# New costs for transfers in a source's list scheduler, other product orders in the middle down stages, and small work moved to another stage

## The chip, the cores and the metric

The kernel runs on one core of a Trainium2 chip. The core has five engines that run side by side, each with its own list of instructions: PE (matrix products into PSUM, a small memory of eight banks), DVE (element-wise work), ACT (element-wise work, copies, activation functions), POOL and SP. Here SP issues the loads of the weights and POOL issues a few transfers that add one on-chip buffer to another. The metric is the time of one execution on the device, in microseconds (us).

## The reference

One layer of a decoder block over 256 tokens of width 2048, in float32:

```
def swiglu_ffn(x, w_gate, w_up, w_down):
    return (jax.nn.silu(x @ w_gate) * (x @ w_up)) @ w_down
...
x = x + 0.5 * swiglu_ffn(rms_norm(x, ffn1_norm), ffn1_w_gate, ffn1_w_up, ffn1_w_down)
z = rms_norm(x, mix_norm) @ w_in
...
a = jnp.exp(-8 * r * jax.nn.softplus(-lam))
...
x = x + y @ w_out
x = x + 0.5 * swiglu_ffn(rms_norm(x, ffn2_norm), ffn2_w_gate, ffn2_w_up, ffn2_w_down)
return rms_norm(x, final_norm)
```

The gate and up weights of an FFN are 2048 x 5632, the down weight is 5632 x 2048. Between the two FFNs lies a mixer (a gated linear recurrence and a short convolution); its vector `softplus(-lam)` and a few others depend on parameters alone and are worked out once by `prepare()`.

## The kernel before

**Products in float32.** A weight block of 512 x 512 (1 MB) is loaded to a buffer `raw`, then split in two parts that PE can multiply: ACT casts `hi` (two instructions of 128x1024), DVE subtracts to get `lo`. Each block is multiplied as `hi` x (both parts of the activations) and `lo` x (the high part). PE needs `hi` first and `lo` right after it.

**Seven products for eight.** Two units of 512 rows and two column blocks form a 2 x 2 matrix of blocks w11, w12, w21, w22, and a scheme after Strassen and Winograd makes its result with seven products p0 to p6 of sums of blocks: p0 uses w11, then w11 takes in w12 (p4), then w22 (p5), then w21 (p3); p6 uses w12 + w22, p2 uses w22 and p1 w21. Two of the sums (w12 += w22 and, in the middle down stages, w11 += w21) are made by POOL transfers, `by_transfer`; the others are DVE additions into the buffer. Beside the seven, ordinary units x01, x11, x00, x10 multiply two more row units; the second digit is the column block. Results gather in PSUM banks named a, c, d, e (and f), each one a 128 x 512 quadrant or part of it. ACT's snapshots of a bank are u2, u3, s5; its copy d<-a (`seed`) lets a bank go on from another's sum. `hs` are sums of activations that some products use; `ph` are PE transposes of a unit of hidden values, and `h` the parts made from them.

**Stages.** Each FFN runs: a first gate/up block; `down(False)`, the down product of units 0, 1, 2 (column block c = 0 as ordinary units d_1_0, then blocks 1 and 2 by seven products, then c = 3 as ordinary units 3_0, 3_2, 3_1, used on PE in that order of 0 first); a fine gate/up stage (g1, u1, g2, u2); `down_stage`, the middle down stage, in two passes d_2_0 and d_2_1 of two column blocks each; a second fine stage (g3, u3, g4, u4); `down(True)`. The number before the first underscore in a name is the FFN: `d1_2_0` is FFN1's middle down stage, pass 0.

**What sets the order.** The fine and middle down stages are laid out by a list scheduler in the source, class `Plan`, that runs when the program is written. A step has an engine, a length, a tail (time until its result is there), and needs; PE's order is fixed by the caller (`usual_order`, `orders`), SP's follows from when a load is late, and the rest is chosen by earliest start and urgency. Loads choose a buffer (`room`) by when its last reader is done; `finish` hands those times to the next stage's plan. In these stages the instructions are pinned to the written order. The other stages are ordered by the framework from dependencies, with the order of the source as priority. For c = 3 of `down(False)` the buffers are named by hand: `chosen["raw"]` gives raw3 to 3_0, which held w11 (last read by p3's split); raw4 held w12 (last read by p6's split). In the buffer rooms of the two layouts, "three" (raw0 to raw4) and "fine" (kept, tall, short), the same memory is used again.

`prepare()` first runs `turns` (two PE transposes, `pv_many` and `pv_conv`, of small parameter rows, each copied by DVE to `cols_many`, `cols_conv`), then on ACT `lam_abs` and `lam_exp` (the latter with another activation table, so an ACT_TABLE_LOAD ahead of it), then some 20 DVE instructions on 128x8 values (`lam_den`, `lam_s`, `lam_poly`, `sp2`, `sn4` and others).

All instructions that go through the wrapper `Engine` have line L43 in the profile, so groups are told apart by names: the profile writes `hi_d_p` for `hi` of a product of a down stage, `hi_d_x` for that of an ordinary unit there, `hi_d` for that of the single units of `down`, `ps_d_a` for a bank, `raw_d_w` for a buffer.

Of the kernel before, what the change touches and what calls it, by code (L numbers as in the profile page):

```python
# [48 lines left out]
class Step:  # L49

    def __init__(self, engine, length, fn, needs, tail, due, at):
        self.engine, self.length, self.fn, self.tail, self.due, self.at = engine, length, fn, tail, due, at
        self.needs = [n for n in needs if n is not None]
        self.late = self.start = self.end = None
        self.room, self.readers = None, []


class Plan:
# [15 lines left out]

    def load(self, length, fn, room, tail=2.3):
        step = self.add("SP", length, fn, tail=tail)
        step.room = room
        return step
# [50 lines left out]
    def run(self):  # L129
# [6 lines left out]
        while True:  # L136
# [37 lines left out]
def hybrid_block(ctx: ExitStack, tc: tile.TileContext, a: dict, out: bass.AP):  # L174
# [94 lines left out]
    turns = []  # L269
# [464 lines left out]
    def ffn(tag, norm, after, opening=False):  # L734
        with tc.tile_pool(name=f"ffn{tag}", bufs=1, side="left", reuse_waits="tile") as fp:
# [304 lines left out]
            def down(last):  # L1040
# [11 lines left out]
                def finish(c, ps):  # L1052
                    y = [keep(f"y_{t}") for t in range(NT)]
                    for t in range(NT):
# [4 lines left out]
                        else:  # L1059
                            for h in range(2):  # L1060
# [3 lines left out]
                                close(t, y[t], h, 2)  # L1064

                for c in (0, 3):
                    if c == 3:
                        chosen["pair"].extend([1, 0, 1, 2][4 - len(us) :])
                        if len(us) == 3:
                            chosen["raw"].extend([3] + [i for i in recent["raw"] if i in (1, 2)])  # L1070
                    end = last and tag == 2 and c == NC_D - 1
# [11 lines left out]
                    if c == 0:  # L1083
# [192 lines left out]
            def fetch(plan, w, cs, runs, name, rooms):  # L1276
                got = {}

                def run(room):
                    rows = sum(n for _, n in runs)  # L1280
                    raw = got["raw"] = pools[room].tile([P, rows, CW], F32, tag="raw", name=f"raw_{name}")
                    at = 0
                    for k, n in runs:
                        sp.dma_start(raw[:, at : at + n, :], w[k * P : (k + n) * P, cs].rearrange("(j p) c -> p j c", p=P))
                        at += n

                step = plan.load(sum(n for _, n in runs) * 0.73, run, rooms)
                return step, lambda: got["raw"]
# [30 lines left out]

            def sevens(plan, w, cs, name, sf, rows, xs, rooms, order, pairs, result, turned4=False, fills=None, apart=False):  # L1320

# [51 lines left out]
                def unit(key):  # L1373
# [13 lines left out]
                    elif key == "p3":  # L1387
                        last = made["p5"].lo[-1]
                        if turned4:
                            sources = [by_transfer("w11", "w21", last, loads["w21"])]  # L1390
# [20 lines left out]
                for key in units_only:  # L1411
                    for n in {"p0": "a", "p5": "a", "p6": "a", "p3": "a", "p4": "f" if apart else "c", "p2": "c", "p1": "d"}.get(key) or (
                        "ec" if key[2] == "1" else "da"
                    ):
                        last_on[n] = key
                wait_for = {
                    (1, 1): ("e", ["u3"] if apart else ["u3", "s5"]), (0, 1): ("c", ["u2"]), (1, 0): ("a", []), (0, 0): ("d", []),
                }
# [8 lines left out]
                for key in order:  # L1427
# [7 lines left out]
                    if key[0] == "x":  # L1435
# [15 lines left out]
                    needs = {5: ["seed"], 6: ["u2"], 3: ["u3"], 2: [] if apart else ["s5"], 1: ["seed"]}.get(q, [])  # L1451
                    u.over(to(b), lambda q=q: sf[q], q in (0, 4), *[made[z] for z in needs], *((fills or {}).get(q, [])))
                    u.under((to(b), lambda q=q: sf[q], q in (0, 4, 5, 6) or last_on[b] == key))
# [60 lines left out]
            def down_result(plan, cols, later, then=None):  # L1514
                def result(t, n, ps, done, keys, snaps, made):
# [58 lines left out]
            def down_stage(s, free, ready, tails, later):  # L1574
# [55 lines left out]
                pairs = [0, 1, 2] * 5 + [0, 1, 2, 1, 0, 1, 2]  # L1630
                orders = [list(usual_order), usual_order[:8] + ["p3", "p1", "x10"]]
                orders[0] = ["x01", lambda: turn_cells(plan, cells, turned), "p0", "x11", "p4", "p1", "p5", "p6", "x00", "p2", "p3", "x10"]
                for i, cols in enumerate(((2 * CW, CW), (3 * CW, 0))):

                    class Late(dict):
# [8 lines left out]
                        plan, wd, cols, f"d{tag}_{s}_{i}", sh, rows, xs, rooms, orders[i], pairs[11 * i : 11 * i + 11],  # L1644
                        down_result(plan, cols, handed if i else None), turned4=True, fills=fills,
                        apart=i == 0,
                    )
# [15 lines left out]
            for s in (1, 3):  # L1663
# [29 lines left out]
    def prepare():  # L1693
        for t in turns:
            t()

        lam = vec["lru_lambda"]
# [479 lines left out]
```

## Time and profile before

| | us |
|---|---|
| Time, median of 3 runs | 1751.11 |
| Lowest and highest | 1747.46, 1751.56 |
| The profiled execution's own time | 1748.15 |
| Its span | 1746.4 |
| PE busy | 1715.0 (98%) |
| DVE busy | 1530.6 (88%) |
| ACT busy | 1096.0 (63%) |
| Mean granted PE clock | 0.996 |

In the timelines below a row is: start, length, engine, line, operation, result <- operands, tile and shape, how many were joined, and in brackets the idle time of the engine before it with what ended it. `SPq` and `POOLq` are the issuing of transfers, and a transfer's row gives its size and the median time from issue to landing. In a table by windows, each engine has its busy time and instructions, and then come the granted clock (1.00 is full speed), the busy share of the DMA engines and the rate.

### The profile page before, as it was taken

To read this page: it belongs to the slowest core of one execution; us is meant where nothing else is said; L and a number is where in the kernel's file an instruction comes from. 1 tells how busy PE (TensorE), PEld (TensorE's weight loads), DVE (VectorE), ACT (ScalarE), POOL (GpSimd) and SP (SyncE) were. 2 spreads that over 40 slices of the span, in tenths; PEclk is the share of its full clock that TensorE was granted. 3 is DMA by queue.
4 is the path that set the end of the run, shared out by engine and by line. 5 is a ranking of instruction groups with operands and counts; after the bars stand their busy time and mean duration, and the time that the engine had idled before them with its cause. 6 is when DMAs were issued, how large, how long until landed. Compare 5 with 4: busy or idle time off the path is not lost. (4 is left out here: it accounts for less than half of the span.)

```text
span 1746.4 us, 20389 instructions
## 1 busy us (share of the span) xinstructions
PE 1715.0 (98%) x7913; PEld 1420.4 (81%) x7913; DVE 1530.6 (88%) x1320; ACT 1096.0 (63%) x1346; POOL 50.8 (3%) x84
## 2 busy tenths in 40 slices
PE   9999999999899999999999999999999999999998
PEld 8888888887688888888888888787888877878886
DVE  7989899997799987887897888788899998999976
ACT  7666566665566655667865666565566565666654
POOL 0100000000000000000000000000000000000000
PEclk9999999999999999999999999999999999999999
DMA  8775976868777865655566675665777877877663
GB/s 299 235 223 165 290 226 221 262 175 268 219 230 226 264 194 193 230 168 183 179 199 207 209 251 158 194 239 152 242 246 229 262 211 233 271 251 227 226 197 121
DMA packets 182450, 383.09 MB, mean 219 GB/s; under 512 B 7509, under 2 KB 10449, under 8 KB 177873
## 3 DMA queue, kind: packets, MB, share of 16 engines
q1 hardware_dynamic: 174656, 340.81, 56.5%
q0 software_dynamic: 7520, 39.92, 11.8%
q8 instruction: 62, 1.02, 0.2%
q10 hardware_dynamic: 176, 1.06, 0.1%
q14 instruction: 36, 0.29, 0.0%
HBM read 339.82 MB, written 2.10 MB: 196 GB/s over the span
## 5 line engine op out<-in xcount | busy, mean ns | idle before, releaser
L43 ACT CAST hi_g_p<-raw_g_w 128x1024 fp32r<-128x1024 f32 x112 | 138.9, 1262 | 85.3 <-DVE raw_g_w L43 36.9
L43 ACT CAST hi_u_p<-raw_u_w 128x1024 fp32r<-128x1024 f32 x112 | 138.3, 1261 | 77.6 <-PE ps_u_a L43 25.8
L43 DVE TENSOR_TENSOR lo_g_p<-raw_g_w,hi_g_p 128x2560 fp32r<-128x2560 f32 (+2 forms) x72 | 159.7, 2227 | 18.8 <-PE ps_d L43 9.7
L43 DVE TENSOR_TENSOR lo_u_p<-raw_u_w,hi_u_p 128x2560 fp32r<-128x2560 f32 (+2 forms) x72 | 159.0, 2227 | 9.6 <-ACT hi_u_p L43 5.9
L43 PE MATMUL ps_in<-xT_nm,hi_in 128*128 128x512 f32 x512 | 122.5, 391 | 0.0
L43 PE MATMUL ps_d<-hi_d,h 128*128 128x512 f32 x440 | 107.0, 396 | 5.0 <-ACT hi_d L43 5.0
L43 PEld LDWEIGHTS ps_in<-xT_nm,hi_in 128*128 128x128 f32 x512 | 94.1, 188 | 18.8 <-ACT tha L43 0.5
L43 PEld LDWEIGHTS ps_d<-hi_d,h 128*128 128x128 f32 x440 | 83.1, 190 | 22.9 <-ACT hi_d L43 5.8
L43 DVE TENSOR_TENSOR lo_in<-raw_in,hi_in 128x2048 fp32r<-128x2048 f32 x32 | 73.2, 2289 | 20.8 <-ACT hi_in L43 20.3
L43 ACT CAST hi_in<-raw_in 128x1024 fp32r<-128x1024 f32 x64 | 64.3, 1047 | 33.6 <-PE ps_in L43 18.2
L43 ACT CAST hi_d<-raw_d 128x1024 fp32r<-128x1024 f32 x56 | 55.5, 1046 | 40.9 <-PE ps_d_d L43 11.5
L43 ACT CAST hi_d_p<-raw_d 128x1024 fp32r<-128x1024 f32 x56 | 56.4, 1046 | 31.6 <-DVE raw_d L43 16.8
L43 DVE TENSOR_TENSOR raw_u_w<-raw_u_w,raw_u_w 128x1024 f32<-128x1024 f32 (+2 forms) x40 | 69.6, 1757 | 6.8 <-DMA raw_u_w<-in_ffn_w_up_dram 5.8
L43 DVE TENSOR_TENSOR lo_d_p<-raw_d,hi_d_p 128x2048 fp32r<-128x2048 f32 x28 | 63.4, 2285 | 10.9 <-ACT hi_d_p L43 10.7
L43 DVE TENSOR_TENSOR lo_d<-raw_d,hi_d 128x2048 fp32r<-128x2048 f32 x28 | 63.6, 2287 | 9.4 <-ACT hi_d L43 9.3
L43 DVE TENSOR_TENSOR lo_d_p<-raw_d_w,hi_d_p 128x2048 fp32r<-128x2048 f32 (+1 forms) x36 | 64.7, 1812 | 6.7 <-ACT hi_d_p L43 6.7
L43 DVE TENSOR_TENSOR raw_g_w<-raw_g_w,raw_g_w 128x1024 f32<-128x1024 f32 (+2 forms) x40 | 69.5, 1754 | 0.9 <-DMA raw_g_w<-in_ffn_w_gate_dram 0.4
L43 ACT CAST hi_d_p<-raw_d_w 128x1024 fp32r<-128x1024 f32 x56 | 56.9, 1047 | 18.5 <-DVE raw_d_w L43 9.3
L43 PEld LDWEIGHTS ps_in<-xT_nm,lo_in 128*128 128x128 f32 x512 | 65.6, 191 | 2.5
L43 PE MATMUL ps_in<-xT_nm,lo_in 128*128 128x256 f32 x512 | 66.4, 283 | 0.0
L43 ACT CAST hi_g_x<-raw_g_x 128x1536 fp32r<-128x1536 f32 x32 | 47.2, 1475 | 25.0 <-DMA raw_g_x<-in_ffn_w_gate_dram 21.2
L43 PE MATMUL ps_g_a<-hi_g_p,x 128*128 128x512 f32 x224 | 58.3, 398 | 2.8 <-ACT hi_g_p L43 2.8
(525 smaller groups left out, 4261.0 us busy)
## 6 DMA issues: line engine op xcount, KB each, us to landing
raw_d<-in_ffn_w_down_dram SPq DMA_DIRECT2D x56, 1024.0 KB, 5.2
raw_g_w<-in_ffn_w_gate_dram SPq DMA_DIRECT2D x32, 1024.0 KB, 6.8
raw_u_w<-in_ffn_w_up_dram SPq DMA_DIRECT2D x32, 1024.0 KB, 6.9
raw_in<-in_w_in_dram SPq DMA_DIRECT2D x32, 1024.0 KB, 5.1
raw_g_x<-in_ffn_w_gate_dram SPq DMA_DIRECT2D x32, 768.0 KB, 7.7
raw_u_x<-in_ffn_w_up_dram SPq DMA_DIRECT2D x32, 768.0 KB, 7.9
raw_u<-in_ffn_w_up_dram SPq DMA_DIRECT2D x23, 1024.0 KB, 5.7
raw_g<-in_ffn_w_gate_dram SPq DMA_DIRECT2D x22, 1024.0 KB, 5.4
```

The lines of the kernel that those rows point to most:

```text
L43: ins = getattr(self.engine, name)(*args, **kwargs)
```

## The change

It has four parts, and the same arithmetic but for the place of one product.

1. The scheduler's costs. A load was a step of 0.73 us for each 128 rows on SP with a tail of 2.3 us. Now it is 0.45 us on SP with a tail of 1.95 + 0.68 us for each, and besides loads and POOL transfers take turns on one common line "DMA", where a load takes 0.67 us for each 128 rows and a transfer of 512 rows 5.3 us. So loads that are issued together, or during a transfer, are reckoned to land one after the other.
2. In the middle down stages p4 no longer goes to a bank of its own (f, in pass 0) or to c (in pass 1), but to e, which becomes quadrant (1,1) with it; ACT copies e into c after p4, and the ordinary units are added to both. The updates of `xres` from f, and from s5 in pass 1, go. x01, which began bank e before, now waits for that copy.
3. Both passes have other orders of units (`down_orders`).
4. `prepare` moves from between FFN1's middle down stage and its second fine stage to `down(True)` of FFN1 in the source, and `turns` to the start of FFN1's `down(False)`. Neither place is pinned. And 3_0 of `down(False)` takes raw4 instead of raw3.

```diff
@@ Plan
-    def load(self, length, fn, room, tail=2.3):
-        step = self.add("SP", length, fn, tail=tail)
-        step.room = room
+    def load(self, rows, fn, room):
+        step = self.add("SP", 0.45, fn, tail=1.95 + 0.68 * rows)
+        step.room, step.share = room, 0.67 * rows
         return step
...
             step.end = begin + step.length + step.tail + 0.07
+            if step.share is not None:
+                step.end = max(step.end, self.free.get("DMA", self.EARLY) + step.share)
+                self.free["DMA"] = step.end
@@ down
+                if tag == 1:
+                    for fn in [prepare] if last else turns:
+                        fn()
                 for c in (0, 3):
                     if c == 3:
                         chosen["pair"].extend([1, 0, 1, 2][4 - len(us) :])
                         if len(us) == 3:
-                            chosen["raw"].extend([3] + [i for i in recent["raw"] if i in (1, 2)])
+                            chosen["raw"].extend([4] + [i for i in recent["raw"] if i in (1, 2)])
...
-                        if tag == 1 and m == 5:
-                            prepare()
@@ sevens
                 def by_transfer(key, other, *needs):
-                    z = plan.add("POOL", 1.0 + five, lambda: moved(key, other), *needs, tail=8.5)
+                    z = plan.add("POOL", 1.0 + five, lambda: moved(key, other), *needs, tail=7.4 + 0.3 * five)
+                    z.share = 5.3 + 1.3 * five
...
                         for b, t in targets:
                             needs = list(ready[t])
-                            fresh = b == "e" or b == "c" and apart
+                            fresh = b == "e" and not down
                             if not fresh:
-                                needs.append(made[{"c": "s5", "d": "seed", "a": "u3"}[b]])
+                                needs.append(made[{"e": "s5", "c": "s5", "d": "seed", "a": "u3"}[b]])
...
-                    b = {0: "a", 5: "a", 6: "a", 3: "a", 4: "f" if apart else "c", 2: "c", 1: "d"}[q]
+                    b = {0: "a", 5: "a", 6: "a", 3: "a", 4: "e" if down else "c", 2: "c", 1: "d"}[q]
...
-                    elif q == 4 and apart:
-                        made["f"] = to("f"), u.low
+                    elif q == 4 and down:
+                        made["s5"] = plan.add("ACT", copy_ps, lambda: act.copy(to("c")(), to("e")()), u.low)
@@ down_result
-                    if keys and "f" in made:
-                        ps4, done4 = made["f"]
-                        plan.add("DVE", add_ps, lambda: update(c, t, ps4()), done4, due=9.0)
@@ before fine_stage
+            down_orders = (
+                ["p0", "p4", "x01", "x11", "p5", "p1", "p6", "x00", "p3", "x10", "p2"],
+                ["p0", "p4", "x01", "p2", "p5", "x11", "p6", "p1", "p3", "x00", "x10"],
+            )
@@ down_stage
-                orders = [list(usual_order), usual_order[:8] + ["p3", "p1", "x10"]]
-                orders[0] = ["x01", lambda: turn_cells(plan, cells, turned), "p0", "x11", "p4", "p1", "p5", "p6", "x00", "p2", "p3", "x10"]
+                orders = [list(z) for z in down_orders]
+                orders[0].insert(2, lambda: turn_cells(plan, cells, turned))
@@ end of the loop over stages
-                    if tag == 1:
-                        prepare()
@@ prepare
     def prepare():
-        for t in turns:
-            t()
-
```

The first place is ACT at the end of FFN1's middle down stage and the start of its second fine stage, where `hi_g1_3_p0` is the first cast of the fine stage. Before:

```order
L43 CAST hi_d1_2_1_x10_3362<-raw_d1_2_1_x10_3315 128x1024 x2
L43 CAST hi_d1_2_1_p1_3383<-raw_d1_2_1_w21_3236 128x1024 x2
L43 ACTIVATE lam_abs_3445<-cols_many_800 128x8
L43 ACT_TABLE_LOAD
L43 ACTIVATE lam_exp_3446<-lam_abs_3445 128x8
L43 CAST hi_g1_3_p0_3510<-raw_g1_3_w11_3504 128x1024
```

Now the same stretch, in which the casts follow each other:

```order
L43 ACTIVATE u3_d1_2_1_3365<-ps_d1_2_1_a_3188 128x512
L43 CAST hi_d1_2_1_x10_3353<-raw_d1_2_1_x10_3297 128x1024
L43 CAST hi_d1_2_1_x00_3372<-raw_d1_2_1_x00_3266 128x1024 x2
L43 CAST hi_g1_3_p0_3480<-raw_g1_3_w11_3474 128x1024
L43 CAST hi_g1_3_p0_3480<-raw_g1_3_w11_3474 128x1536
```

And ACT where those instructions stand now, in FFN1's first down stage, between the casts of c = 0 (`hi_d1_1_0_...`) and of the first of the seven products:

```order
L43 CAST hi_d1_1_0_2_1240<-raw_d1_1_0_2_1238 128x1024 x2
L43 CAST hi_d1_1_0_1_1271<-raw_d1_1_0_1_1269 128x1024
L43 ACTIVATE lam_abs_4660<-cols_many_800 128x8
L43 ACT_TABLE_LOAD
L43 ACTIVATE lam_exp_4661<-lam_abs_4660 128x8
L43 CAST hi_d1_1_p0_1334<-raw_d1_1_40_1322 128x1024 x2
L43 CAST h1_1_1221<-ph1_1_1_1222 128x4x128
```

The three instructions have moved from the head of a stage's first cast to the middle of an earlier stage, ahead of `hi_d1_1_p0` and the casts of `h1_1`.

The second place is SP at the end of FFN2's first down stage. Before, 3_0 is the last load of that stage:

```order
L43 DMA raw_d2_1_00_9440<-in_ffn2_w_down_dram 128x4x512
L43 DMA raw_d2_1_80_9442<-in_ffn2_w_down_dram 128x4x512
L43 DMA raw_d2_1_3_2_9679<-in_ffn2_w_down_dram 128x4x512
L43 DMA raw_d2_1_3_1_9710<-in_ffn2_w_down_dram 128x4x512
L43 DMA raw_d2_1_3_0_9648<-in_ffn2_w_down_dram 128x4x512
```

Now:

```order
L43 DMA raw_d2_1_00_9436<-in_ffn2_w_down_dram 128x4x512
L43 DMA raw_d2_1_80_9438<-in_ffn2_w_down_dram 128x4x512
L43 DMA raw_d2_1_3_0_9644<-in_ffn2_w_down_dram 128x4x512
L43 DMA raw_d2_1_3_2_9675<-in_ffn2_w_down_dram 128x4x512
L43 DMA raw_d2_1_3_1_9706<-in_ffn2_w_down_dram 128x4x512
```

3_0 has moved ahead of 3_2 and 3_1 (in FFN1, where it stood between them, ahead of 3_2).

The third place is ACT in pass 1 of FFN1's middle down stage, around the copies out of banks. Before:

```order
L43 CAST hi_d1_2_1_p0_3129<-raw_d1_2_1_w11_3078 128x1024 x2
L43 CAST hi_d1_2_1_x01_3178<-raw_d1_2_1_x01_3120 128x1024
L43 CAST hi_d1_2_1_p4_3180<-raw_d1_2_1_w11_3078 128x1024
L43 CAST hi_d1_2_1_x01_3178<-raw_d1_2_1_x01_3120 128x1024
L43 CAST hi_d1_2_1_p4_3180<-raw_d1_2_1_w11_3078 128x1024
L43 COPY ps_d1_2_1_d_3212<-ps_d1_2_1_a_3183 128x512
L43 CAST hi_d1_2_1_x11_3221<-raw_d1_2_1_x11_3158 128x1024
L43 ACTIVATE s5_d1_2_1_3232<-ps_d1_2_1_c_3203 128x512
```

Now:

```order
L43 CAST hi_d1_2_1_p0_3141<-raw_d1_2_1_w11_3078 128x1024 x2
L43 CAST hi_d1_2_1_p4_3177<-raw_d1_2_1_w11_3078 128x1024 x2
L43 CAST hi_d1_2_1_x01_3197<-raw_d1_2_1_x01_3122 128x1024 x2
L43 CAST hi_d1_2_1_p2_3207<-raw_d1_2_1_w22_3145 128x1024 x2
L43 COPY ps_d1_2_1_d_3226<-ps_d1_2_1_a_3188 128x512
L43 COPY ps_d1_2_1_c_3228<-ps_d1_2_1_e_3209 128x512
L43 CAST hi_d1_2_1_p5_3243<-raw_d1_2_1_w11_3078 128x1024
L43 CAST hi_d1_2_1_x11_3262<-raw_d1_2_1_x11_3158 128x1024
```

The snapshot s5 has become the copy c<-e, and it stands behind the casts of x01 and of p2, which is now the unit after x01.

More of the change, by code (lines that the diff above doesn't have):

```diff
@@ L54, in __init__ @@
         self.late = self.start = self.end = None
-        self.room, self.readers = None, []
+        self.room, self.readers, self.share = None, [], None
 class Plan:
@@ L1285, in run @@
                         at += n
-                step = plan.load(sum(n for _, n in runs) * 0.73, run, rooms)
+                step = plan.load(sum(n for _, n in runs), run, rooms)
                 return step, lambda: got["raw"]
@@ L1318, in turn_item, with sevens @@
                 return turned_parts(plan, high, low, a)
-            def sevens(plan, w, cs, name, sf, rows, xs, rooms, order, pairs, result, turned4=False, fills=None, apart=False):
+            def sevens(plan, w, cs, name, sf, rows, xs, rooms, order, pairs, result, fills=None, down=False):
                 bank_of, snaps = {}, {}
@@ L1388, in unit @@
                         last = made["p5"].lo[-1]
-                        if turned4:
+                        if down:
                             sources = [by_transfer("w11", "w21", last, loads["w21"])]
@@ L1411, in sevens @@
                 for key in units_only:
-                    for n in {"p0": "a", "p5": "a", "p6": "a", "p3": "a", "p4": "f" if apart else "c", "p2": "c", "p1": "d"}.get(key) or (
+                    for n in {"p0": "a", "p5": "a", "p6": "a", "p3": "a", "p4": "e" if down else "c", "p2": "c", "p1": "d"}.get(key) or (
                         "ec" if key[2] == "1" else "da"
@@ L1416, in sevens @@
                 wait_for = {
-                    (1, 1): ("e", ["u3"] if apart else ["u3", "s5"]), (0, 1): ("c", ["u2"]), (1, 0): ("a", []), (0, 0): ("d", []),
+                    (1, 1): ("e", ["u3"] if down else ["u3", "s5"]), (0, 1): ("c", ["u2"]), (1, 0): ("a", []), (0, 0): ("d", []),
                 }
@@ L1449, in sevens @@
                     q = int(key[1])
-                    b = {0: "a", 5: "a", 6: "a", 3: "a", 4: "f" if apart else "c", 2: "c", 1: "d"}[q]
-                    needs = {5: ["seed"], 6: ["u2"], 3: ["u3"], 2: [] if apart else ["s5"], 1: ["seed"]}.get(q, [])
+                    b = {0: "a", 5: "a", 6: "a", 3: "a", 4: "e" if down else "c", 2: "c", 1: "d"}[q]
+                    needs = {5: ["seed"], 6: ["u2"], 3: ["u3"], 2: ["s5"], 1: ["seed"]}.get(q, [])
                     u.over(to(b), lambda q=q: sf[q], q in (0, 4), *[made[z] for z in needs], *((fills or {}).get(q, [])))
-                    u.under((to(b), lambda q=q: sf[q], q in (0, 4, 5, 6) or last_on[b] == key))
+                    u.under((to(b), lambda q=q: sf[q], q in (0, 5, 6) or q == 4 and not down or last_on[b] == key))
                     if q == 0:
                         made["seed"] = plan.add("ACT", copy_ps, lambda: act.copy(to("d")(), to("a")()), u.low)
-                    elif q == 4 and apart:
-                        made["f"] = to("f"), u.low
+                    elif q == 4 and down:
+                        made["s5"] = plan.add("ACT", copy_ps, lambda: act.copy(to("c")(), to("e")()), u.low)
                     elif q == 4:
```

3 lines of the change are left out of this document (1 added, 2 removed).

## The prediction

> **What bounds the kernel now.** I read the page's first part, then the waits of PE, then the timelines around the longest of them. The page says who works:
>
> ```profile
> PE 1715.0 (98%) x7913; PEld 1420.4 (81%) x7913; DVE 1530.6 (88%) x1320; ACT 1096.0 (63%) x1346; POOL 50.8 (3%) x84
> ```
>
> PE has work in all but 31 us of the 1746.4 us span, and the change takes no matmul away. So only PE's waits can move the time. The waits of PE, grouped by who ends them (total us, times, longest):
>
> ```profile
> PE ps_d L43 <- ACT hi_d L43: 5.0, 2, 4.0
> PE ps_g_a L43 <- ACT hi_g_p L43: 2.8, 1, 2.8
> PE ps_u_c L43 <- ACT hi_u_p L43: 2.7, 1, 2.7
> PE ps_d_a L43 <- DVE lo_d_p L43: 1.8, 2, 1.1
> PE ps_g_c L43 <- ACT hi_g_p L43: 1.8, 2, 1.0
> PE ps_g_c L43 <- ACT s_g L43: 1.5, 1, 1.5
> PE ps_d_a L43 <- ACT u_d L43: 1.5, 2, 0.7
> PE ps_d_d L43 <- DVE lo_d_p L43: 1.4, 2, 0.7
> ```
>
> These make 18.5 us. The question is which of them sit where the change works, and which others it adds. Some cost twice: in the windows view the columns are busy time of each engine, then the granted clock, DMA share and GB/s.
>
> ```profile
> 456.00:459.50 3.50, 3.48 (x9) 2.68 (x10) 3.16 (x12) 1.34 (x1) 0.00 (x0) 0.52 1.05 387
> 1125.00:1128.60 3.60, 3.60 (x10) 2.79 (x9) 3.56 (x3) 0.64 (x2) 0.01 (x1) 0.53 0.92 182
> 1217.20:1220.60 3.40, 3.40 (x9) 2.63 (x10) 3.40 (x3) 0.81 (x1) 0.00 (x0) 0.52 0.41 151
> 460.00:475.00 15.00, 10.55 (x41) 7.31 (x41) 14.90 (x12) 10.66 (x10) 1.75 (x2) 1.00 0.61 138
> 1480.00:1500.00 20.00, 20.00 (x90) 16.48 (x89) 18.04 (x13) 10.42 (x10) 1.75 (x2) 1.00 1.05 335
> ```
>
> Right behind the waits of 2.8, 2.7 and 4.0 us the granted clock is 0.52 for about 3.5 us, which loses 3.5 x 0.48 = 1.7 us each; behind the shorter waits (460 to 475) it is 1.00.
>
> **1. `prepare` leaves the start of FFN1's stage 3.** Around 456 us PE, DVE and ACT read:
>
> ```profile
> 456.02 4.14 PE L43 MATMUL ps_g_a<-hi_g_p,x 128*128 128x512 f32 x10 [2.83 <-ACT hi_g_p L43]
> 453.02 0.24 DVE L43 COPY cols_many<-pv_many 128x80 f32<-128x80 f32 x1 [6.82 <-PE pv_many L43]
> 456.11 1.57 DVE L43 SCALAR_TENSOR_TENSOR lam_poly<-lam_poly,lam_s 128x8 f32<-128x8 f32 x8
> 458.02 2.83 DVE L43 TENSOR_TENSOR lo_g_p<-raw_g_w,hi_g_p 128x2560 fp32r<-128x2560 f32 x1
> 453.30 0.21 ACT L43 ACTIVATE lam_abs<-cols_many 128x8 f32<-128x8 f32 x1 [11.06 <-DVE cols_many L43]
> 453.53 1.28 ACT L43 ACT_TABLE_LOAD   x1
> 454.94 2.40 ACT L43 CAST hi_g_p<-raw_g_w 128x1024 fp32r<-128x1024 f32 x2
> ```
>
> DVE stands idle for 6.82 us and ACT for 11.06 us until PE reaches the transposes `pv_many`, although the split of the next weights could have run: the instructions are pinned in that order. Then ACT does `lam_abs`, a table load and `lam_exp` before the first cast, and DVE its chain of small ones until 458.02 before the first `lo_g_p`. PE pays 2.83 us, and in 460 to 475 another 15.00 - 10.55 = 4.45 us while DVE catches up: 7.28 us, and 1.7 us of clock. What is left without `prepare` is shown by FFN2, which has the same transition and no `prepare`: in 1480 to 1500 PE is busy for all 20.00 us. Gain 9.0 us.
>
> The same work now lies in FFN1's first down stage, unpinned. The two transposes cost PE what they cost before. ACT gets 0.21 + 1.28 + 0.21 = 1.7 us ahead of `hi_d1_1_p0`; DVE gets two copies and some 20 small instructions of about 0.2 us (1.57 us for 8), 4.5 us. The tightest follower is h1_1, which PE needs for the third unit:
>
> ```profile
> 144.64 1.28 DVE L43 TENSOR_TENSOR h<-ph,h 128x512 fp32r<-128x512 f32 x2
> 148.67 3.79 PE L43 MATMUL ps_d<-hi_d,h 128*128 128x512 f32 x16
> ```
>
> It was ready at 145.9. Now its casts stand behind the table load, and its residual on DVE behind `lo_d1_1_p0`, whose cast is later by the same 1.7 us; I get 148.4 against 149.1 (148.67 and the transposes). That is 0.7 us of room. DVE then runs about 1.4 us later up to the middle product's sums. Price 0 to 6.2 us (all 1.7 + 4.5 on the path); I take 0.7, nearer the lower end because h1_1 still fits.
>
> **2. `raw4` for the first unit of c = 3 (3_0).**
>
> ```profile
> 185.75 3.92 PE L43 MATMUL ps_d<-hi_d,h 128*128 128x512 f32 x16 [0.96 <-ACT hi_d L43]
> 1217.12 5.51 PE L43 MATMUL ps_d<-hi_d,h 128*128 128x512 f32 x16 [4.00 <-ACT hi_d L43]
> 1216.02 1.99 ACT L43 CAST hi_d<-raw_d 128x1024 fp32r<-128x1024 f32 x2 [1.41 <-DMA raw_d<-in_ffn_w_down_dram]
> 1210.67 0.37 SPq L43 DMA_DIRECT2D raw_d<-in_ffn_w_down_dram  x1
> 1191.99 6.69 DVE L43 TENSOR_TENSOR lo_d_p<-raw_d,hi_d_p 128x2048 fp32r<-128x2048 f32 x3 [0.26 <-PE ps_d_c L43]
> ```
>
> In FFN2 the load of 3_0 goes out at 1210.67, because raw3 holds the first quadrant until its last split; its cast waits for it and PE waits 4.00 us. raw4 held the second quadrant, free at the latest when that group of three splits ends, 1198.7. Issued there, with the 5.3 us that this load took (1210.67 to 1216.0), it lands by 1204; PE's product before c = 3 ends at 1213.1. So the wait goes: 4.00 + 1.7 of clock = 5.7 us. 3_2 and 3_1, whose rooms were free earlier, now go out behind it; they are used one and two units of 5.5 us after it, so 5.3 us a load keeps pace. In FFN1 0.96 us goes. What is late next is the first load of the gate stage behind raw4: it now waits for 3_0's split, still two units of 5.6 us ahead of its own use; hidden by those, and 0 to 2 us if not. I take 0. Gain 6.7 us.
>
> **3. Middle down stages: order and banks.** The waits there:
>
> ```profile
> 389.63 2.11 PE L43 MATMUL ps_d_a<-hi_d_p,hs 128*128 128x512 f32 x8 [0.73 <-ACT u_d L43]
> 404.38 0.96 PE L43 MATMUL ps_d_a<-lo_d_p,h 128*128 128x512 f32 x3 [1.14 <-DVE lo_d_p L43]
> 446.26 1.19 PE L43 MATMUL ps_d_d<-lo_d_p,h 128*128 128x512 f32 x4 [0.68 <-DVE lo_d_p L43]
> 1423.19 2.11 PE L43 MATMUL ps_d_a<-hi_d_p,hs 128*128 128x512 f32 x8 [0.73 <-ACT u_d L43]
> 1436.86 1.19 PE L43 MATMUL ps_d_a<-lo_d_p,h 128*128 128x512 f32 x4 [0.68 <-DVE lo_d_p L43]
> 388.99 0.59 ACT L43 ACTIVATE u_d<-ps_d_a 128x512 f32<-128x512 f32 x1
> 376.26 0.58 ACT L43 COPY ps_d_d<-ps_d_a 128x512 f32<-128x512 f32 x1
> 371.40 1.04 PE L43 MATMUL ph<-ident,z 128*128 128x128 f32 x8
> 389.33 1.28 DVE L43 SCALAR_TENSOR_TENSOR xres<-ps_d_f,xres 128x512 f32<-128x512 f32 x2
> raw_d_x<-in_ffn_w_down_dram SPq DMA_DIRECT2D x3, 1024.0 KB, 9.5
> raw_d_w<-raw_d_w POOLq DMA_DIRECT2D x2, 1024.0 KB, 8.4
> ```
>
> Removed: in pass 0 p6 overwrote bank a right after p5, so PE waited 0.73 us for the copy `u_d` of 0.59 us; now p1 stands between them (3 us of PE). The waits of 1.14 and 0.68 us belong to loads and splits at the seam of the passes and at the end of pass 1, and the new orders put other units there; the rooms of the first two quadrants of pass 1 come free earlier. I let them go: 0.73 + 1.14 + 0.68 in FFN1, 0.73 + 0.68 in FFN2, 3.96 together. The xres adds that go from DVE (1.28 us in pass 0, one of them in pass 1) were off PE's path: 0.
>
> Added: x01 goes on in the bank that p4 filled, so it waits until ACT has copied e into c. In pass 0 the transposes `ph` (0.8 us of PE) stand between and cover a copy of 0.58 us, 0 to 0.1. In pass 1 nothing stands between; the nearest row is the same pattern, a copy out of a bank that PE wants next, 0.73 us. In both, ACT must be there: copy c<-e is issued behind the casts of x01 and x11, four of 1.0 us from 367.7, when p0 has freed their buffers by my count: 371.7. p4 ends at 371.4, since p0 and p4 together are as long as x01 was (`ph` started at 371.40). So 0.7 to 2 us for each FFN; I take 0.83. Net gain 3.96 - 1.66 = 2.3 us.
>
> The pass-0 load that is late next is w21: its room is x01's, free only after `lo_x01`, about 372.8, while a POOL transfer (8.4 us) runs from 367.6 to 376 (my estimate: it follows the sum of the first two quadrants, which p0 in front lets end that early). Alone a load takes 5.3 us; the loads of this stage that met a transfer took 9.5: it lands at 378.1 to 382.3. `hi_p1` stands on ACT ahead of the second half of p5's cast, so that half is ready 2.0 + 0.6 + 1.05 us later, 381.8 to 386.0, and PE wants it at about 384.0. 0 to 2.0 us for each FFN; I take 0.6, since the transfer is more than half done by then.
>
> [...]
>
> **4. The planner's new costs for loads and transfers.** They change places by one or two on ACT and DVE in the fine stages, with PE's order there the same; I followed the three moved casts and found each done before PE asks. 0, with 0 to 1 us for each of four stages.
>
> **The sum.** 9.0 - 0.7 + 6.7 + 2.3 - 1.2 = 16.1 us. The profiled execution took 1748.15 us, so 1732 on its scale. The runs shown were 1747.46, 1751.11 and 1751.56, their median 3.0 us above the profiled one; half of that for the scale of a median gives 1733.5.
>
> **Rivals.**
> (a) `prepare`'s work stalls FFN1's first down stage, all 6.2 us of it: 1739. For it: DVE has about 0.7 us of room at h1_1. Against: DVE and ACT have idle stretches there and only h1_1 is tight.
> (b) Other loads become late once the waits go; PE was slack for them. If half of the gain comes back as waits for loads: 1741.5. For it: DMA share is 1.05 at some seams. Against: 1480 to 1500 ran full at that share.
> (c) The half clock does not come from the waits. Then the 3.4 us of clock in the sum stay: 1737. [...] The trace has half clock behind all three waits over 2.6 us and behind none of up to 1.48.
> (d) Slower: w21 lands so late in both pass 0s that p5 waits. To undo 16 us it must land 8 us beyond my upper end, at 390 or later, with the clock halved behind it; its own transfer p3 hangs on that too. Then 1750 to 1760.
> (e) The wait at 456 was for the load and not for `prepare`, so 9 us stay: 1742. Against: the casts follow `lam_exp` without a gap.
>
> **Chances.** Forecast 0.63, (a) 0.13, (b) 0.12, (c) 0.04, (d) 0.04, (e) 0.04. Upper end: (b) and the median's scale, 1743; lower end: sum without the allowances of 0.7 and 1.2 us, and the clock stretch at 1125 gone by chance, 1728. The forecast's own range is 1729 to 1739. About 0.3% (5.3 us) is what a measurement can tell from no change; faster by more: the forecast, (a), (c), and most of (b) and (e), 0.91; within 0.06, slower 0.03.
>
> **What would show it.** Right: in the waits of PE `hi_d` falls from 5.0 to under 0.5, `hi_g_p` on g_a is gone, the only half-clock stretch left is near 1120; new rows for x01 behind the copy c<-e, 0.7 us each; 3_0's load ahead of 3_2 about 12 us earlier. Wrong: waits for `hi_d_p` in pass 0, for h or the split in FFN1's first down stage, or for loads at a seam, each of 3 us or more.

## The result and the profile after

The changed kernel takes 1724.35 us (median of four runs, 1723.03 to 1725.56), the kernel before 1751.22 us on the same chip: a ratio of 0.9851, 95% interval 0.9834 to 0.9868. Run again on another chip beside the last experiments it took 1725.45 against 1749.18 us, 0.9865 (0.9846 to 0.9883). The forecast of 1733.5 us had the direction and the larger causes, and its range ended too high, at 1728. The profiled execution took 1725.39 us with a span of 1723.6 us, 22.8 us less than that of before; its page and the waits of PE (total us, times, longest):

```profile
PE 1708.0 (99%) x7913; PEld 1421.1 (82%) x7913; DVE 1527.3 (89%) x1314; ACT 1097.9 (64%) x1348; POOL 50.8 (3%) x84
```

```profile
PE ps_u_c L43 <- ACT hi_u_p L43: 2.7, 1, 2.7
PE ps_d_c L43 <- ACT s_d L43: 1.7, 1, 1.7
PE ps_d_e L43 <- ACT ps_d_c L43: 1.3, 2, 0.7
PE idle L43 <- DVE ones L43: 1.1, 1, 1.1
PE pb_n L43 <- DVE diag_n L43: 0.4, 1, 0.4
```

All waits of `hi_d`, `hi_g_p`, `lo_d_p`, `s_g` and `u_d` are gone, and two of 0.66 us for the copy c<-e have come. The whole list sums to 7.4 us, before to 22.8. PE's busy time fell by 7.0 us with the same 7913 products. The places that the prediction spoke of, in the timeline of PE, and the window over the old stall:

```profile
450.48 2.43 PE L43 MATMUL ps_g_a<-hi_g_p,x 128*128 128x512 f32 x10
1200.20 3.79 PE L43 MATMUL ps_d<-hi_d,h 128*128 128x512 f32 x16
...
413.22 1.09 PE L43 MATMUL ps_d_e<-lo_d_p,hs 128*128 128x512 f32 x4
414.97 2.11 PE L43 MATMUL ps_d_e<-hi_d_x,h 128*128 128x512 f32 x8 [0.66 <-ACT ps_d_c L43]
416.92 1.99 PE L43 MATMUL ps_d_c<-hi_d_x,h 128*128 128x512 f32 x8
418.74 1.07 PE L43 MATMUL ps_d_e<-lo_d_x,h 128*128 128x512 f32 x4
419.65 1.07 PE L43 MATMUL ps_d_c<-lo_d_x,h 128*128 128x512 f32 x4
```

```profile
446.00:472.00 26.00, 26.00 (x116) 21.53 (x115) 25.11 (x17) 16.44 (x15) 1.75 (x2) 1.00 0.95 298
1111.80:1115.20 3.40, 3.37 (x9) 2.65 (x10) 3.37 (x3) 0.93 (x1) 0.35 (x1) 0.61 0.79 154
```

The first gate product of stage 3 follows without a wait, c = 3 of FFN2 too, and the only half clock left between the start and the end is behind the wait near 1112 us, which the change does not touch.

The rows at 413 to 420 also show what a wait costs beside its idle time. Four products normally take 0.91 us from start to start (418.74 to 419.65) and eight 1.82 (416.92 to 418.74). Here the four take 1.75 us, with the 0.66 us of idleness, and the first eight behind the wait 1.95. Together that is 0.84 + 0.13 = 0.97 us for a wait listed with 0.66: 0.3 us more. The row at 418.74 ends at 419.81, 0.16 us behind the start of the next, while that at 413.22 ended at 414.31, 0.66 us ahead of the next.

So I measured PE's delays from start to start: for each product, the time to the next start less 0.227 us, the commonest distance between products of 512 columns in both traces (0.113 for 256 columns, half of it, where 0.120 is the commonest), summed over a place. In us:

| place | before | after | gain | forecast |
|---|---|---|---|---|
| first 12 us | 3.0 | 4.9 | -1.9 | 0 |
| FFN1, first down stage | 1.6 | 0.3 | 1.3 | 0.3 |
| FFN1, middle down stage up to 445 | 3.0 | 0.9 | 2.0 | 0.4 |
| 446 to 472 | 11.5 | 0 | 11.5 | 9.7 |
| FFN2, c = 3 of the first down stage | 5.9 | 0 | 5.9 | 5.7 |
| FFN2, middle down stage | 2.9 | 0.9 | 2.0 | 0.0 |
| FFN2, fine stages | 1.6 | 0 | 1.6 | 0 |
| FFN2, last down stage | 1.2 | 1.9 | -0.8 | 0 |
| all else | 16.0 | 15.0 | 1.0 | 0 |
| sum | 46.6 | 24.0 | 22.6 | 16.1 |

### The profile page after: what moved, and what is told of

It is laid out like the page before. It is cut to its first block, busy times and chain, and to the rows that moved or that the text cites. A ratio compares the mean times of both kernels' runs of the same rounds, so it can differ in the third digit from the quotient of the medians.

```text
span 1723.6 us, 20401 instructions
## 1 busy us (share of the span) xinstructions
PE 1708.0 (99%) x7913; PEld 1421.1 (82%) x7913; DVE 1527.3 (89%) x1314; ACT 1097.9 (64%) x1348; POOL 50.8 (3%) x84
## 3 DMA queue, kind: packets, MB, share of 16 engines
q0 software_dynamic: 7520, 39.92, 11.9%
## 4 chain that ended last, share of the span: by engine, by line
PE 95%; DVE 2%; ACT 1%; DMA 1%; issue 1%; DVEq 0%; ACTq 0%
PE ps_in L43 10%; PE ps_u_a L43 10%; PE ps_g_a L43 10%; PE ps_d L43 9%; PE ps_d_a L43 7%; PE ps_u_c L43 6%; PE ps_g_c L43 6%; PE ps_u_d L43 4%; PE ps_d_c L43 4%; PE ps_g_d L43 4%; PE ps_d_d L43 3%; PE ps_d_e L43 3%; PE ps_u_e L43 3%; PE ps_o L43 3%; PE ps_g_e L43 3%; PE ps_g L43 2%
## 5 line engine op out<-in xcount | busy, mean ns | idle before, releaser
L43 ACT CAST hi_g_p<-raw_g_w 128x1024 fp32r<-128x1024 f32 (+1 forms) x112 | 139.2, 1263 | 93.6 <-DVE raw_g_w L43 31.9
L43 ACT CAST hi_d<-raw_d 128x1024 fp32r<-128x1024 f32 x56 | 55.5, 1047 | 39.3 <-PE ps_d_d L43 11.5
L43 DVE TENSOR_TENSOR lo_g_x<-raw_g_x,hi_g_x 128x1536 fp32r<-128x1536 f32 x32 | 56.1, 1754 | 4.6 <-ACT hi_g_x L43 4.6
L43 PE MATMUL ps_u_a<-hi_u_p,x 128*128 128x512 f32 x224 | 57.1, 391 | 0.0
```

The costliest lines, as they stand in the source:

```text
L43: ins = getattr(self.engine, name)(*args, **kwargs)
```

## The experiments

**`prepare` alone.** The kernel before with `prepare` in FFN1's `down(True)` and `turns` in its `down(False)`, as in the change.

```diff
+                if tag == 1:
+                    for fn in [prepare] if last else turns:
+                        fn()
                 for c in (0, 3):
...
-                    if tag == 1:
-                        prepare()
```

> The kernel before with part 4's first half alone: `prepare` in the last down stage of FFN1, `turns` at the start of its first. Theory 1 (a wait of PE costs its idle time and about 0.27 us more, since the first product behind it is longer and no longer overlaps its predecessor; half clock comes with waits over 2.6 us): the six waits between 455 and 472 us go, 7.28 + 6 x 0.27 + 1.7 of clock = 10.6 us, time about 1740.6, and no new wait of over 0.3 us in FFN1's first down stage. Theory 2 (my sum's terms were right for their parts and the surplus comes from elsewhere): 8.3 us, time about 1743. Rival (a) of the prediction: 3 us or less saved, with new waits in FFN1's first down stage.

It took 1743.23 us against 1750.48, ratio 0.9958 (0.9944 to 0.9973), 7.3 us less: less than theory 1 gave and near theory 2's number, but not for theory 2's reason. The stall at 455 to 472 is gone, and the waits of PE from 425 to 475 us read:

```profile
PE ps_d_d L43 <- ACT hi_d_x L43: 1.9, 1, 1.9
```

Against 0.95 us of delay at the end of pass 1 before, there are now 3.7 (this wait, its 0.3 us and half clock behind it, 0.61 on the average from 439.2 to 443.0 us): ACT stands for 10.0 us until the load of x00 is there. That load goes out close to the last POOL transfer of the pass. The transfer went out 1.6 us ahead of it before and 0.3 us ahead of it here; the two loads and the transfer there, before and then here:

```profile
raw_d_x<-in_ffn_w_down_dram SPq DMA_DIRECT2D x2, 1024.0 KB, 9.4
raw_d_w<-raw_d_w POOLq DMA_DIRECT2D x1, 1024.0 KB, 8.2
```

```profile
raw_d_x<-in_ffn_w_down_dram SPq DMA_DIRECT2D x2, 1024.0 KB, 11.7
raw_d_w<-raw_d_w POOLq DMA_DIRECT2D x1, 1024.0 KB, 11.4
```

Why the transfer went out later is not shown; the old stall, which lies behind this place, cannot have hidden it. Nothing of over 0.3 us appears in FFN1's first down stage beside the old wait of c = 3, so rival (a) falls. In the changed kernel the same work reads, on ACT and DVE there:

```profile
142.27 0.20 ACT L43 ACTIVATE lam_abs<-cols_many 128x8 f32<-128x8 f32 x1
142.50 1.28 ACT L43 ACT_TABLE_LOAD   x1
143.79 0.21 ACT L43 ACTIVATE lam_exp<-lam_abs 128x8 f32<-128x8 f32 x1
143.91 1.98 ACT L43 CAST hi_d_p<-raw_d 128x1024 fp32r<-128x1024 f32 x2
```

```profile
148.14 1.28 DVE L43 TENSOR_TENSOR h<-ph,h 128x512 fp32r<-128x512 f32 x2
```

h1_1 was ready at 149.4, and PE, 2.5 us later than before by then (1.9 of it from the start), did not wait.

**`turns` alone.** The kernel before with the two transposes at the start of FFN1's first down stage, and `prepare` where it was.

```diff
+                if tag == 1 and not last:
+                    for fn in turns:
+                        fn()
                 for c in (0, 3):
...
     def prepare():
-        for t in turns:
-            t()
-
```

> The kernel before with only `turns` (the two PE transposes and, with them, their copies) at the start of FFN1's first down stage; `prepare`'s ACT and DVE work keeps its place in the source between the middle down stage and stage 3. Theory 3 (the stall of 456 us comes from the transposes, which find a place on PE only at the end of the stage; the small work is not pinned and goes into gaps of ACT and DVE as soon as its input is there): the stall goes as with the whole move, 10.5 us less at 450 to 472 us. Theory 4 (the small work itself makes the stall, 1.7 us on ACT and 4.5 us on DVE ahead of the stage's first splits): at least half of it stays there, waits of 3 us or more.

1742.3 us against 1749.43, 0.9957 (0.9945 to 0.9969): the same as the whole move. In the profiled execution 9.7 us of delay went at the old stall, and some 3 us came in small waits elsewhere. `lam_abs` and `lam_exp`, still written behind the middle down stage, ran at 140.64 and 142.16 us, as soon as their input was there. PE's waits from 425 to 475 us:

```profile
PE ps_d_d L43 <- DVE lo_d_p L43: 0.8, 1, 0.8
PE ps_g_c L43 <- ACT s_g L43: 0.7, 1, 0.7
PE ps_d_d L43 <- ACT hi_d_x L43: 0.4, 1, 0.4
```

Theory 3 holds for the stall. The small work was never pinned; what held it back was its input, two short PE transposes that the framework had put at the end of the stage.

**raw4 alone.**

```diff
-                            chosen["raw"].extend([3] + [i for i in recent["raw"] if i in (1, 2)])
+                            chosen["raw"].extend([4] + [i for i in recent["raw"] if i in (1, 2)])
```

> The kernel before with raw4 in place of raw3 for unit 3_0, nothing else. Theory 1: the waits of 0.96 and 4.00 us go, 4.96 + 2 x 0.27 + 1.6 of clock = 7.1 us, time about 1744. Theory 2: 6.7 us. These two differ by too little for the time; what the run decides is whether the whole of it comes from this edit, without the new costs and orders.

1742.61 us against 1750.48, 0.9958 (0.9945 to 0.9971), 7.9 us less. Both waits for `hi_d` are gone, and the delays of 1.23 and 5.87 us at these places with them; the whole of it comes from this one number.

**Middle down stages alone.** The changed kernel with the old costs, raw3 and `prepare` in its old place, that is, the kernel before with the new banks and orders. This kernel does not compute the same result. My guess at the cause is the bank of one quadrant (d of FFN1's stage g3), which held `pv_many`, 80 columns wide, right before ACT copied a start into it; no run shows it. PE has the same 7913 products.

```diff
-                orders = [list(usual_order), usual_order[:8] + ["p3", "p1", "x10"]]
+                orders = [list(z) for z in down_orders]
+                orders[0].insert(2, lambda: turn_cells(plan, cells, turned))
...
-                    b = {0: "a", 5: "a", 6: "a", 3: "a", 4: "f" if apart else "c", 2: "c", 1: "d"}[q]
+                    b = {0: "a", 5: "a", 6: "a", 3: "a", 4: "e" if down else "c", 2: "c", 1: "d"}[q]
```

> The kernel before with the middle down stages of the change alone: p4 in bank e and the new unit orders, with the old costs of loads and transfers, `prepare` and raw3 as before. Theory 1: waits of 0.73, 0.30, 1.14, 0.68 us in FFN1 and 0.73, 0.68, 0.73 in FFN2 go, 4.99 + 7 x 0.27 = 6.9 us, and two waits for the copy of e come, 2 x (0.66 + 0.27) = 1.9 us; 5.0 us saved, time about 1746. Theory 2: 1.1 to 2.3 us saved. If the orders need the new costs, waits for loads show in these stages and less than 3 us is saved.

1733.3 us against 1750.48, 0.9899 (0.9884 to 0.9914): 17.2 us, where theory 1 gave 5.0. The waits of the middle down stages behave as theory 1 said. But the stall of 456 us went as well, with `prepare` in its old place in the source. PE in pass 1, and the window over the old stall:

```profile
414.77 0.23 PE L43 MATMUL pv_many<-ident,rows_many 80*128 80x80 f32 x1
414.94 0.27 PE L43 MATMUL pv_conv<-ident,rows_conv 56*128 56x56 f32 x1
415.59 2.12 PE L43 MATMUL ps_d_e<-hi_d_x,h 128*128 128x512 f32 x8 [0.39 <-ACT ps_d_c L43]
```

```profile
452.00:475.00 23.00, 22.73 (x100) 18.50 (x99) 20.36 (x13) 15.60 (x15) 0.29 (x1) 1.00 0.81 227
```

The wait for the copy c<-e leaves a gap on PE in the middle of pass 1, and the transposes now run in it, 38 us sooner than before. Why the framework takes this gap, and in the kernel before did not take that of 1.14 us at 404 us, is not shown. So the new orders and the move of `prepare` both remove the same stall, some 10.6 of the 11.5 us in the table, and the parts do not add up.

**Costs alone.**

```diff
-                step = plan.load(sum(n for _, n in runs) * 0.73, run, rooms)
+                step = plan.load(sum(n for _, n in runs), run, rooms)
...
+                    z.share = 5.3 + 1.3 * five
```

> The kernel before with the scheduler's new costs alone. Theory 1: three waits of FFN2's second fine stage (0.03, 0.39 and 0.34 us) are set by the order that the costs give, and go: 0.76 + 3 x 0.27 = 1.6 us, time about 1749.6. Theory 2, and my forecast for this part: 0, those waits stay, and in the changed kernel they go because the stage starts at another point. The middle down stages with their old orders could change by up to 1 us either way.

1748.86 us against 1750.48, 0.9994 (0.9984 to 1.0003): not to be told from no change. In the trace the three small waits of FFN2's fine stages are gone, as theory 1 had it, and FFN1's pass 0 lost its waits for loads; but with the old orders FFN2's pass 1 got a new one, where the load went out together with the transfer, which took 11.9 us:

```profile
1471.25 2.07 PE L43 MATMUL ps_d_d<-hi_d_x,h 128*128 128x512 f32 x4 [4.35 <-ACT hi_d_x L43]
```

**The change without the costs.** The changed kernel with the old lengths and tails of loads and transfers.

> The changed kernel with the old costs of loads and transfers. Theory 5 (the new orders stand without the new costs, which only take the small waits of the fine stages): 1724.4 + 0.5 to 2 us, with waits of 0.2 to 0.4 us at the starts of the fine stages and none for loads in the middle down stages. Theory 6 (the orders need the costs): waits for loads of 1 us or more in the middle down stages, 3 us or more slower than the changed kernel.

1726.52 us against 1749.43, 0.9867 (0.9849 to 0.9885). Theory 5: no wait for a load in the middle down stages, one of 0.45 us in a fine stage. The small waits of FFN2's fine stages are gone here too, so the new costs are not needed for that.

**The change without the orders.** The changed kernel with the old orders and banks.

> The changed kernel with the middle down stages of before (bank f, old orders); costs, `prepare` and raw4 as changed. Theory 7 (parts add up as they were alone: 7.3, 7.9 and 1.6 us): time about 1733.7, with waits for loads of 3 us and more at the end of pass 1 in one or both FFNs, as the move of `prepare` alone and the costs alone showed them. Theory 8 (the old stages cost only the waits they had, 4.99 + 7 x 0.27 - 1.9 = 5.0 us): about 1729.4.

1736.83 us against 1749.43, 0.9927 (0.9911 to 0.9942), so the orders and banks are worth some 12 us once everything else is changed. Theory 7's 1733.7 is nearer than theory 8's 1729.4, and both are too low. PE's waits and ACT at the end of FFN1's pass 1:

```profile
PE ps_d_d L43 <- ACT hi_d_x L43: 4.7, 1, 4.7
```

```profile
433.93 1.99 ACT L43 CAST hi_d_p<-raw_d_w 128x1024 fp32r<-128x1024 f32 x2 [10.50 <-DMA raw_d_w<-raw_d_w]
435.82 0.59 ACT L43 ACTIVATE u_d<-ps_d_a 128x512 f32<-128x512 f32 x1
436.31 3.87 ACT L43 CAST hi_d_x<-raw_d_x 128x1024 fp32r<-128x1024 f32 x4
```

ACT stands for 10.5 us until a POOL transfer ends, with the casts of x00 queued behind that one. 7.4 us of delay for PE here: the wait, and half clock, with eight products in 3.78 us behind it where eight took 1.99 at 416.92 in the changed kernel. The transfer went out 0.65 us behind the load of x00 and took 11.6 us. Before, it took 8.2 us in FFN1 and 8.3 in FFN2 where it led the load by 1.6 and 1.4 us; with `prepare` alone 11.4 us at a lead of 0.3 us, and with the costs alone 11.9 us where the load went out together with it. In the changed kernel it leads by 1.9 us in both FFNs and takes 8.1 us.

**Orders without the new banks.** As the last, with `down_orders` in.

> The changed kernel with the banks of before in the middle down stages (p4 in f or c, s5 by a snapshot, the xres adds on DVE back) and only the new unit orders kept. Theory 9 (the orders alone carry the gain of these stages, since they let rooms go sooner; the bank scheme costs two waits): no waits for loads in these stages, the two waits for the copy c<-e gone, 2 x (0.66 + 0.27) = 1.9 us less than the changed kernel. Theory 10 (the new orders need the bank scheme, since DVE's three more adds in each stage make splits late): waits of 0.5 us or more for splits in the middle down stages, and no gain or a loss against the changed kernel.

1724.71 us, beside 1725.45 for the changed kernel on the same chip, ratios to before 0.9864 (0.9848 to 0.9879) and 0.9865. The two waits for the copy are gone and others came, 0.60 us in FFN1's pass 0 and these in FFN2's:

```profile
1396.27 0.50 PE L43 MATMUL ps_d_a<-hi_d_p,hs 128*128 128x512 f32 x1 [2.12 <-ACT hs L43]
1397.61 2.93 PE L43 MATMUL ps_d_a<-hi_d_p,hs 128*128 128x512 f32 x7 [0.84 <-DVE hs L43]
```

```profile
1391.29 2.94 ACT L43 CAST hi_d_p<-raw_d_w 128x1024 fp32r<-128x1024 f32 x3 [7.37 <-DMA raw_d_w<-in_ffn_w_down_dram]
1394.14 0.61 ACT L43 CAST hs<-hv 128x512 fp32r<-128x512 f32 x1
```

ACT waits 7.4 us for the load of w21, and the activations' sum that p5 needs stands behind its casts: that is the mechanism of rival (d), in this kernel with 5 us of delay. Theory 9 holds for what carries the gain (the orders), theory 10 for the price, though a load and not DVE's adds makes it: no net gain without the new banks.

**A better version.** The changed kernel, with raw4 for w11 and raw3 for w12 in FFN2's first up block; then also with the updates of column block 0 behind the snapshots in FFN2's last down stage; then that with the old banks; and the changed kernel once more.

```diff
-        w11, w12 = get(r0, 0, "kept0"), get(r0, 1, "kept1")
+        w11, w12 = get(r0, 0, "kept1" if swap else "kept0"), get(r0, 1, "kept0" if swap else "kept1")
...
                         def others(i):
+                            if i == 0 and last and tag == 2:
+                                for fn in first:
+                                    fn()
```

> The changed kernel, and in FFN2's first up block the first two quadrants change rooms: w11 goes to raw4, free early, and w12 to raw3, the same fault as c = 3 had. If the wait of 2.68 us near 1112 us comes from w11's load (ACT waits for it until 1103.1), it goes with its clock and refill, 4.5 us: 1719.9. If DVE's order there (lo of p0, a sum of the gate, then w11 + w12) makes it, 2 us or more of it stay. Either way nothing may appear in the first down stage of FFN2, whose first quadrants take over these rooms.

> The kernel of the run with swapped rooms (4 us faster than the changed kernel), and in FFN2's last down stage the updates of column block 0, with the squares for the final norm that ACT does on them, come after the snapshots s1 and s5 in the source. If ACT's 3.4 us of standing still for those squares makes the wait of 1.7 to 2.0 us near 1655 us, that goes: 1.9 us, or 3.8 us where the wait had half clock behind it; time about 1717 to 1718.5. If the casts behind make it, it stays.

> The last two together: the banks of before with the new orders, the swapped rooms and the later updates. By theory 9 another 1.9 us below the run before it, 1715 to 1717; by theory 10 not below it.

> The changed kernel again, beside the next three on one chip: 1724 to 1726, with waits of 0.66 us for the copy c<-e in pass 1 of both FFNs, 2.68 us near 1112 and 1.7 us near 1659.

The swapped rooms took 1720.45 us against 1749.43, 0.9835 (0.9819 to 0.9852): the wait of 2.68 us and the half clock behind it are gone, so it was the load. With the later updates 1718.84 us (1718.2 to 1720.7) against 1749.18, 0.9831 (0.9816 to 0.9845), where the changed kernel on that chip had 1721.56 to 1726.94. That is the lowest time, not to be told from the swapped rooms alone by the ratios. Its second edit did not do what it was for:

```profile
1653.43 1.89 PE L43 MATMUL ps_d_c<-hi_d_x,h 128*128 128x512 f32 x7 [1.46 <-ACT s_d L43]
```

The wait stays, with the squares still ahead of the snapshot on ACT, so what makes it stays open. With the old banks it was 1722.94 us, 0.9853 (0.9839 to 0.9868), again with waits for `hs` in FFN2's pass 0.

## Why the prediction was wrong

Right: that PE's waits decide, where they sit, and what ends them. Point 2 (raw4) came out as worked out, 5.9 against 5.7 us in FFN2. The new waits for the copy came at 0.66 us in pass 1 of both FFNs and none in pass 0, as taken. Rivals (b), (d) and (e) did not come, and (a) left no trace. (c) did not come either, since both half clocks went with their waits; its doubt on what brings them was sound in so far as the length of a wait alone does not decide (last section).

Wrong was the size of the sum, 16.1 us where the profiled executions differ by 22.8. The step that failed is the price of a wait:

- I summed idle times. Each wait costs 0.3 us more (0.27 on the average), and 21 waits became 7: 3.8 us. So the premise that only the idle time can move does not hold: PE's busy time fell by 7.0 us, with 1.6 us of clock behind each of two waits and in spite of the slower start. The extra is in most rows of the table above, above all in the stall at 446 to 472 (seven waits) and in the middle down stages.
- In the middle down stages I also overlooked two waits. One is of 0.30 us at 401, whose row I did not show. The row `ps_d_d <- DVE lo_d_p` says two times, and I counted only the one at 446; the other, 0.73 us, is at the end of FFN2's pass 1 (1.0 us with its 0.3).
- I took 0.6 us for each FFN for the late w21 and 0.7 for `prepare`'s new place. Neither came: 1.9 us. The POOL transfers of that stage took 7.4 us (the row below, from the issues of 360 to 400 us) where I had reckoned 8.4. The one that I had let run to 376 was over at 373.1, before w21's load went out at 373.4; that landed at 378.5, and p5 did not wait.

```profile
raw_d_w<-raw_d_w POOLq DMA_DIRECT2D x2, 1024.0 KB, 7.4
```

- The new costs I put at 0; the small waits of FFN2's fine stages went, 0.8 us and their 0.3 each (the costs alone did the same, and so did the change without them).
- Against that, 0.8 us more at the end and 1.9 us more at the start of the profiled execution (below).

With these terms the sum is 21 of the 22.6 us in the table; the rest lies in many small delays.

Then the scale: before's profiled execution was 3.1 us below its median and after's 1.0 above, so the medians on that chip differ by 26.9 us. I allowed 1.5 us for this. On the other chip the medians differ by 23.7, so I take this part for scatter and no gain; the intervals of the two ratios overlap.

Wrong in its reason, though by luck near in its size, was point 1. I wrote that the instructions are pinned; `turns` alone and the middle down stages alone show that they are not, and that either the move or the new orders would have removed the stall. And I priced the orders as a small term (2.3 us). They are worth some 12 us in the changed kernel, because with the old orders the last transfer of pass 1 and the load beside it go out too close together and become late (the transfer took 11.6 us there; with `prepare` alone transfer and loads took 11.4 and 11.7, before 8.2 and 9.4): rival (b), which the new orders prevent.

## What to carry to other kernels

Price a wait of PE from start to start of its neighbours, not by its idle time, and look at the window behind it for half clock (0.52 and 0.53 over about 3.5 us behind three waits in the kernel before). Look at what goes out close together: a transfer that led a load by 0.3 us took 11.4 us here, and one that led by 1.9 us took 8.1. Parts of a change that each look good alone may share one stall (the four alone give 34 us, together 24 to 27) or may need each other. Before blaming the volume of small work at a stage's seam, ask which single instruction holds its input back: here two transposes of 0.2 us.

## What was not expected of the hardware

**Half clock is not a matter of the wait's length alone.** The trace holds a list of the granted clock. Between start and end it is 0.50 there for 3.41 us at a time: from 456.15, 1125.16 and 1217.33 us in the kernel before, behind waits of 2.83, 2.68 and 4.00 us, and from 1112.53 us in the kernel after, behind one of 2.68. Three windows of as much, each with the window behind it: one with part of a wait of 2.66 us (orders without the new banks), one with part of a wait of 1.91 us (the changed kernel again) and one with the whole of a wait of 1.81 us (the change without the costs). PE's busy time stands behind the comma, and the granted clock is the third number from the end:

```profile
1108.01:1111.42 3.41, 1.61 (x7) 1.35 (x8) 3.41 (x3) 2.00 (x2) 0.86 (x1) 1.00 0.30 60
1111.42:1114.84 3.42, 3.42 (x17) 2.79 (x16) 3.38 (x2) 1.67 (x2) 0.00 (x0) 1.00 1.12 208
```

```profile
1656.78:1660.19 3.41, 2.16 (x9) 1.79 (x10) 3.41 (x4) 3.17 (x5) 0.00 (x0) 1.00 0.84 299
1660.19:1663.60 3.41, 3.41 (x16) 2.81 (x16) 3.41 (x3) 2.00 (x2) 0.00 (x0) 1.00 0.15 17
```

```profile
1658.38:1661.79 3.41, 1.60 (x8) 1.07 (x7) 3.41 (x4) 3.41 (x5) 0.00 (x0) 1.00 0.73 214
1661.79:1665.20 3.41, 3.41 (x10) 2.67 (x9) 3.09 (x3) 2.58 (x4) 0.00 (x0) 0.50 0.24 93
```

The wait near 1110 us had half clock behind it with 2.68 us in the kernel after and none with 2.66 in the first pair, and 1.81 us had it once where 1.91 had not. In the first window of each pair PE stands idle for 1.80, 1.25 and 1.81 us, and the clock of the second is 1.00, 1.00 and 0.50. What decides beside the length of the wait is not shown.

**The start.** The first products of 512 columns lie 0.43 us apart in place of 0.23 for a time that differs from execution to execution: until 9.9 us in the profiled execution of the kernel after, and not beyond 6.2 us in that of the kernel before. Before, and after:

```profile
5.88 1.19 PE L43 MATMUL ps_g<-hi_g,xT_n 128*128 128x512 f32 x4 [0.22 <-ACT hi_g L43]
```

```profile
5.88 2.08 PE L43 MATMUL ps_g<-hi_g,xT_n 128*128 128x512 f32 x4 [0.21 <-ACT hi_g L43]
```

The delays of the first 12 us were 3.0 us before and 4.9 after. From 1 to 11 us PE has 43 products before and 41 with raw4 alone, but 35 after, 35 with `prepare` alone, 35 with the costs alone and 34 with the middle down stages alone. The windows view prints a granted clock of 1.00 there, here in the kernel after:

```profile
1.00:11.00 10.00, 9.73 (x35) 8.23 (x36) 3.54 (x8) 5.07 (x10) 0.29 (x1) 1.00 0.86 290
```

But the list of the granted clock has no entry that early. Its first, of full clock, starts at 5.59 us before and at 10.02 after, and after's products lie 0.43 us apart until then and 0.23 behind. So the 1.00 stands for no record, and 1.9 us of the two delays' difference goes with when that entry starts; the counts above differ among kernels whose edits all lie behind these products, so I take it for scatter.
